# Setting the byte distance between the two operands of every matmul in a two-layer retention and gMLP block

## The chip, the cores and the metric

One NeuronCore of a Trainium2 chip runs the kernel in one launch. The metric is the device time of a whole execution in microseconds (us). The kernel before was timed three times: 915.23, 916.29 and 919.71 us, median 916.29 us.

## The reference

Two residual layers work on 512 latent tokens and 256 context tokens of width 1024. Layer 0 mixes tokens by bidirectional retention in four heads, layer 1 by a chunked gMLP; the result is the latent stream after a last RMSNorm. Cut to what matters:

```python
# layer 0
hx = rmsnorm(x, norm_g[0]) * (1 + scale_x) + shift_x      # hc the same from ctx
q, k, v, z = hx @ w_q, hx @ w_k, hx @ w_v, hx @ w_z       # rope on q, k
o = retention_forward(q, k, v) + retention_backward(q, k, v)   # states start from ctx
x = x + gate_x * ((rms(o) * silu(z)) @ w_out)
# layer 1
h = rmsnorm(x, norm_g[1]) * (1 + scale) + shift
u, v, z = h @ w_u, h @ w_v, h @ w_z
y = u * (w_s . normalised(v) + b_s) * silu(z)
x = x + gate * (y @ w_out);  return rmsnorm(x, final_g)
```

## The kernel before

**Precision.** TensorE takes float32r operands. Nearly every operand is kept as two halves, a rounded high part `h` and a low part `l`, side by side in one SBUF tile. `mm3` (L95) makes a product of three matmuls: low by high, high by low, high by high. In each matmul one operand is loaded into the array (the *stationary* operand, 128 columns, its own LDWEIGHTS in the trace) and the other streams past it (the *moving* operand, 256 or 512 columns). `split` (L101) makes the halves: ScalarE (ACT) copies the high part, VectorE (DVE) subtracts to get the low part.

**Projections.** The big products (q and k together, v, z, and u, v, z of layer 1) are cut in two by two blocks and multiplied with seven block products instead of eight (class `Product`, L298). The activations' blocks and their sums lie in seven 8 KB slots: A11, A12, A22, S1, S2, S3, S4 (tags `oA11` and so on). The context rows lie in a 16 KB slot `hc`. Class `Stream` (L125) brings the weights: it loads a raw block from HBM into a 4 KB slot (`w0` to `w7`, `g0` to `g3` and others, name `raw`), forms a difference where the scheme wants one (on DVE), and splits it into one of four 8 KB slots, tag `hl`. A block in `hl` is used by 24 matmuls, by 48 where the context rows are multiplied with it too.

`features` (L282), for q with k (`kq`) and for u with z (`u`), loads the weights `hl` into the array and streams the activations. `tokens` (L290), for v and z of layer 0 (`vz`) and v of layer 1 (`v1`), does it the other way round: the activations are stationary, the weights `hl` move.

**Retention.** `attend` (L917): `score` multiplies k (stationary) with q (moving, 256 wide) out of five 4 KB slots (name `qk`); `pv` takes the scores' halves `ph`, `pl` (2 KB slots, tag `t2`) as stationary operand and v (512 wide) as the moving one; v lies in the slots of A11, S1 and S2. `project_out` (L1005) has the output weights (`hl`) stationary and the gated result `og` moving; `og` lies in the slots of S3 and S4. `load_qk` (L826) brings q and k of the next head back from DRAM, each piece into a slot that a list of tags names.

**Layer 1's output.** `out1` (L1199) has the gated features stationary, `ya` in the slot `hc` and `yb` in `g2` and `g3`, and the weights `hl` moving, 512 wide.

**Where a tile lies.** Tiles come from one SBUF pool. A tag's slots get their address when the first tile with that tag is asked for, one behind the other, each rounded up to 32 bytes. So small tiles that are made early shift the start of all later ones.

**Order.** The text orders the work on TensorE (PE), ACT and DVE (class `Queue`, L38; through it every instruction of these engines has line L54 in the profile). SyncE (SP) issues all loads in one queue (L114), GpSimd (POOL) all stores to DRAM (L111).

Of the kernel before, what the change touches and what calls it, by code (L numbers as in the profile page):

```python
# [8 lines left out]
F32R = mybir.dt.float32r  # L9
# [4 lines left out]
P = 128  # L14
# [11 lines left out]
TW = XW + CW  # L26
# [41 lines left out]
def hybrid_kernel(ctx, tc, xT_d, cT_d, cv_d, sv_d, rows_d, ada0_d, adag_d, w_d, rope_d, dec_d, ws_d, id_d, out_d):  # L68
# [13 lines left out]
    def st(shape, tag, dt=F32, bufs=1, name=None):  # L82
        return sb.tile(shape, dt, tag=tag, name=name or tag, bufs=bufs)

    T2 = 11

    def t2(name, shape=(P, 512), dt=F32):
        return st(list(shape), "t2", dt, bufs=T2, name=name)

    def pt(shape=(P, 512), tag="ps"):  # L90
        return ps.tile(list(shape), F32, tag=tag, name="pst", bufs=6 if tag == "ps" else 2)
# [9 lines left out]
    def split(hl, src, late=None):  # L101
        h, l = hl
        act.copy(h, src)
        low = lambda: dve.tensor_tensor(l, src, f32(h), ALU.subtract)
        if late is None:
            low()
        else:
            late.append(low)
# [4 lines left out]
    def load(dst, src):  # L113
        nc.sync.dma_start(dst, src)  # L114


    USES = {"B11": ("11",), "B12": ("12",), "T1": ("12", "11"), "T2": ("22", "11"), "B21": ("21",), "T3": ("22", "12"),
            "B22": ("22",), "T4": ("21", "11")}
    AT = {"B11": "11", "B12": "12", "T1": "11", "T2": "11", "B21": "21", "T3": "12", "B22": "22", "T4": "21"}
    WITH = {"B11": "A11", "B21": "A12", "T1": "S1", "T2": "S2", "B22": "S4", "T3": "S3", "T4": "A22"}  # L120
    PAIRED = ("B11", "B21", "T1", "T2", "B22", "T3", "T4")
    SINGLE = ("B11", "T1", "T2", "B21", "T3", "B22", "T4")
    HL = 4

    class Stream:  # L125


# [37 lines left out]
        def upto(self, n, late=None):  # L165

            while self.done < min(n, self.limit or len(self.items)):
                q, name, uses, at, place = self.items[self.done]
                self.pump()
                raw = lambda u: self.raws[q, u]  # L170
                r = raw(at)
                if name[0] == "T":
                    dve.tensor_tensor(r, raw(uses[0]), raw(uses[1]), ALU.subtract)
                elif name[0] == "gated":
                    g = self.gate[:, name[1]:name[1] + 512].unsqueeze(1).to_broadcast([P, 2, 512])
                    rr = r.rearrange("p (e n) -> p e n", e=2)
                    dve.tensor_tensor(rr, rr, g, ALU.mult)
                hl = place() if place else st([P, 2, 1024], "hl", F32R, bufs=HL)
                split((hl[:, 0, :], hl[:, 1, :]), r, late)
                self.tiles[self.done] = hl  # L180
                self.done += 1
                if late is None:
                    self.drop(q, uses)
                else:
                    late.append(lambda: self.drop(q, uses))
# [89 lines left out]
    def op(key):  # L275
        A[key] = st([P, 2, 4, HS], "o" + key, F32R)
# [78 lines left out]
    cv = st([P, KT, 2], "cv")  # L355
# [47 lines left out]
    g0 = sv[:, 32:48].rearrange("p (k r) -> p k r", r=2)  # L403
    gateb0 = sv[:, 48:56]
    adab1 = sv[:, 56:72].rearrange("p (s k) -> p s k", s=2)
    g1 = sv[:, 72:80]
# [51 lines left out]
    def spread(s, name):  # L458

        pr = pt((P, HS), tag="tm")  # L460
        for i in range(2):
            mm(pr[:, i * P:i * P + P], s[:, 1, i:i + 1].to_broadcast([P, P]), ident, start=True, stop=True)
        rs = st([P, HS], name)
        act.copy(rs, pr)
        return rs
# [11 lines left out]
    def ada0_cols(kb, e):  # L477
        pq = pt((P, HS), tag="tm")
        for b in range(2):
            pe.transpose(pq[:, b * P:b * P + P], e[:, b * P:b * P + P], ident)  # L480
        s = st([P, 2, 2], "ada_s", bufs=2)
        v = pq.rearrange("p (b g r) -> p b r g", b=2, g=4)
        dve.tensor_reduce(s, v[:, :, 0:2, :], axis=AX.X, op=ALU.add)
        dve.tensor_tensor(gs0[:, kb, :], s[:, 0, :], adab0[:, 1, kb, :], ALU.add)
        dve.tensor_tensor(sh0[:, kb, :], s[:, 1, :], adab0[:, 0, kb, :], ALU.add)
        dve.scalar_tensor_tensor(gs0[:, kb, :], gs0[:, kb, :], 1.0, g0[:, kb, :], ALU.add, ALU.mult)

    hc = st([P, 2, KT, HS], "hc", F32R)
# [6 lines left out]
    rope = st([P, 2, SEQ], "rope")  # L495
# [53 lines left out]
    rs, sq = {}, {}  # L549

    def half_rows(src, g, s):
        for i in range(2):
            flips(src, g, i, s)
# [11 lines left out]
    def come(*what, then=None):  # L565


        made = []
        for kb, th in what:
            g, k = divmod(kb, 4)  # L570
            r = th // 2
            if r:
                f, h, l = cq[g][:, k, :], hc[:, 0, kb, :], hc[:, 1, kb, :]
            else:
                name = NAMES[th][g]
                if k == 0:
                    A[name] = st([P, 2, 4, HS], AT_S3.get(name, "o" + name), F32R)
                f, h, l = xq[th, g][:, k, :], A[name][:, 0, k, :], A[name][:, 1, k, :]
            dve.scalar_tensor_tensor(f, f, gs0[:, kb, r:r + 1], rs[th], ALU.mult, ALU.mult)
            made.append((f, sh0[:, kb, r:r + 1], h, l))  # L580
        if then:
            then()
        for f, b, h, l in made:
            act.activation(h, f, AF.Identity, bias=b, scale=1.0)
        for f, b, h, l in made:
            dve.scalar_tensor_tensor(l, f, b, f32(h), ALU.add, ALU.subtract)

    w0, bank = {}, {}

    def plain(kb, th, nhs=range(2)):  # L590

        g = kb // 4
        for nh in nhs:
            if th == 0 and kb % 4 == 0:
                w0[g, nh] = Q.get(ahead=0)
        if th == 2:
            if kb == 0:
                bank["c"] = pt()
            features(bank["c"], hc[:, :, 4 * g:4 * g + 4, :], w0[g, 0], g == 0, (kb % 4,))
            return  # L600
        for nh in nhs:
            if kb == 0:
                bank[th, nh] = pt()
            features(bank[th, nh], A[NAMES[th][g]], w0[g, nh], g == 0, (kb % 4,))
# [50 lines left out]
    for kb in range(1, 8):  # L655
        if kb == 3:
            Q.upto(4)
        plain(kb, 0)
        if kb + 1 < 8:
            ada0_cols(kb + 1, es)  # L660
            come((kb + 1, 0), (kb + 1, 1))
        if kb in (2, 6, 7):
            Q.upto({2: 3, 6: 5, 7: 6}[kb])
        plain(kb, 1)
        if kb + 2 < 8:
            es = ada0_mm(kb + 2)
        if kb == 2:
            ada0_load(6)
            ada0_load(7)
            Q.cap = None  # L670
            Q.pump()
        if kb in (2, 3):
            half_rows(rows_c, kb - 2, sq[2])
        if kb == 3:
            inverse(sq[2])
        if kb == 4:
            rs[2] = spread(sq[2], "rs2")
        come(*((k, 2) for k in CTX_COME.get(kb, ())))
        if kb == 7:
            hold((0, 0), (0, 1), (1, 0), (1, 1))  # L680
            op("S1")
            dve.tensor_tensor(f22, f21, f22, ALU.add)
            dve.tensor_tensor(shb, sh0[:, 0:4, 0], sh0[:, 4:8, 0], ALU.add)
            for k in range(4):
                shifted(f22[:, k, :], shb[:, k:k + 1], A["S1"][:, 0, k, :], A["S1"][:, 1, k, :])
        for k in CTX_PLAIN.get(kb, ()):
            plain(k, 2)
# [58 lines left out]
    gate0 = st([P, KT], "gate0")  # L746
# [77 lines left out]
        dve.tensor_tensor(l, f32(l), f32(h), ALU.subtract)  # L824

    def load_qk(h):  # L826
        tags = ("s0", "s1", "s2", "s3", "rope") if h % 2 == 0 else ("w4", "w5", "w6", "g2", "g3")
        srcs = (k_d[h][0], q_d[h][0], k_d[h][1], kc_d[h], q_d[h][1])
        t = []
        for tag, src in zip(tags, srcs):  # L830
            t.append(st([P, 2, 2, HS], tag, F32R, name="qk"))
            load(f32(t[-1][:, 1]).rearrange("p a b -> p (a b)"), src)
            if len(t) % 2:
                yield
        for x in t:
            halves(x)
            yield
        qk[h] = (t[1], t[4]), (t[0], t[2]), t[3]
        yield
# [3 lines left out]
    def load_wo(h):  # L843
        raws = []
        for c in range(4):
            for j in range(len(raws), min(c + 2, 4)):
                raws.append(st([P, 1024], ("w0", "w7")[j % 2], name="raw"))
                load(raws[j], w_d[16 * h + 12 + j])
            if c == 0:
                yield  # L850
            w = st([P, 2, 1024], "hl", F32R, bufs=HL)
            split((w[:, 0, :], w[:, 1, :]), raws[c])
            wos.setdefault(h, []).append(w)
            yield
# [554 lines left out]
```

## Time and profile before

| | |
|---|---|
| profiled execution: span from first to last instruction | 914.7 us |
| runs: median (lowest, highest) | 916.29 us (915.23, 919.71) |
| PE busy | 893.0 us, 98% of the span, 6872 matmuls |
| DVE busy | 722.8 us, 79% |
| ACT busy | 445.5 us, 49% |
| POOL busy | 51.5 us, 6% |
| TensorE clock granted | 0.997 |
| HBM traffic | 167 GB/s over the span |

The median of the runs is 1.6 us above the span of the profiled execution; that much lies around it or differs from run to run. A PE that is busy for 98% is not a PE at its peak: a matmul's record lasts from its start to its modelled end, and the next one starts long before that. What the stream costs is seen from start to start.

### The profile page before, as it was taken

Reading aid. Unit: us, or ns where it says so; the run is one execution under the profiler, and the core shown is the slowest. Engines: PE = TensorE matmul, PEld = TensorE weight load, DVE = VectorE, ACT = ScalarE, POOL = GpSimd, SP = SyncE. Lnnn points to the kernel's source line nnn. Section 1 sums busy time; section 2 is a strip of 40 time slices with the busy share of each in tenths; the row PEclk is TensorE's granted clock in tenths of the full one; section 3 lists DMA queues with packets and bytes.
Section 4 is the critical chain, followed back from the end, with each engine's and each line's share of the span. In section 5 each row is a group of like instructions: output and inputs, shape, how many; then the busy total and the mean of one; then the engine's idle time right before and its main releaser. Section 6 shows DMA issues by size and latency. Waiting matters only on the chain.

```text
span 914.7 us, 16952 instructions
## 1 busy us (share of the span) xinstructions
PE 893.0 (98%) x6872; PEld 846.9 (93%) x6872; DVE 722.8 (79%) x1024; ACT 445.5 (49%) x683; POOL 51.5 (6%) x88
## 2 busy tenths in 40 slices
PE   7999999999999998999999999999999999999997
PEld 6899999999999998998989889999999899899885
DVE  2689977698779866778666759999899489689985
ACT  5464634434545434636264448744545435244244
POOL 0001201101102011000000001011000000000000
PEclk9999999999999999999999999999999999999999
DMA  9943957456666367747254502536335135037102
GB/s 331 387 133 111 315 193 253 150 193 207 209 222 221 126 219 257 273 137 257 102 163 138 184 29 88 176 125 214 133 116 168 39 116 185 24 116 246 54 24 93
DMA packets 76782, 153.81 MB, mean 168 GB/s; under 512 B 7840, under 2 KB 34592, under 8 KB 76704
## 3 DMA queue, kind: packets, MB, share of 16 engines
q1 hardware_dynamic: 69840, 130.70, 43.3%
q0 software_dynamic: 6720, 22.03, 6.4%
q8 instruction: 54, 0.88, 0.4%
q14 instruction: 24, 0.20, 0.1%
q10 hardware_dynamic: 144, 0.01, 0.0%
HBM read 128.58 MB, written 24.12 MB: 167 GB/s over the span
## 4 chain that ended last, share of the span: by engine, by line
PE 82%; DVE 8%; DMA 4%; ACT 3%; issue 2%; SPq 1%; DVEq 0%; ACTq 0%
PE pst L54 82%; DVE hl L54 2%; DVE raw L54 2%; DVE ya L54 1%; DMA acc<-in_xT_dram 1%; DMA xq<-in_xT_dram 1%; ACT hl L54 1%; DMA raw<-in_w_dram 1%; SPq L114 1%; DMA vt<-vt 1%; ACT f L54 1%; ACT junk L54 0%; ACT oA L54 0%; DVE snap L54 0%; DVE bns L54 0%
## 5 line engine op out<-in xcount | busy, mean ns | idle before, releaser
L54 DVE TENSOR_TENSOR hl<-raw,hl 128x1024 fp32r<-128x1024 f32 x195 | 236.5, 1220 | 66.9 <-ACT hl L54 65.8
L54 ACT CAST hl<-raw 128x1024 fp32r<-128x1024 f32 x195 | 202.8, 1049 | 140.5 <-DVE raw L54 67.8
L54 PE MATMUL pst<-oS,hl 128*128 128x256 f32 x1104 | 136.1, 281 | 2.4 <-DVE hl L54 1.8
L54 PE MATMUL pst<-hl,oS 128*128 128x256 f32 x1152 | 137.6, 280 | 0.2 <-DVE snap L54 0.2
L54 PEld LDWEIGHTS pst<-hl,oS 128*128 128x128 f32 x1152 | 136.0, 188 | 1.3 <-ACT snap L54 0.8
L54 PEld LDWEIGHTS pst<-oS,hl 128*128 128x128 f32 x1104 | 132.3, 188 | 4.4 <-ACT ya L54 2.1
L54 PE MATMUL pst<-oA,hl 128*128 128x256 f32 x936 | 120.0, 284 | 0.2
L54 PEld LDWEIGHTS pst<-oA,hl 128*128 128x128 f32 x936 | 114.5, 189 | 2.5 <-DVE raw L54 0.8
L54 DVE TENSOR_TENSOR raw<-raw 128x1024 f32<-128x1024 f32 x92 | 111.3, 1219 | 0.8
L54 PE MATMUL pst<-hl,oA 128*128 128x256 f32 x816 | 100.3, 281 | 0.0
L54 ACT COPY snap<-pst 128x512 f32<-128x512 f32 x92 | 53.8, 585 | 95.0 <-PE pst L54 94.7
L54 PEld LDWEIGHTS pst<-hl,oA 128*128 128x128 f32 x816 | 98.0, 189 | 0.1
L54 PE MATMUL pst<-og,hl 128*128 128x256 f32 x768 | 93.7, 282 | 0.0
L54 PEld LDWEIGHTS pst<-og,hl 128*128 128x128 f32 x768 | 91.6, 188 | 0.9 <-DVE acc L54 0.2
L54 PE MATMUL pst<-hl,ya 128*128 128x512 f32 x288 | 70.3, 395 | 2.2 <-DVE ya L54 2.2
L54 PEld LDWEIGHTS pst<-hl,ya 128*128 128x128 f32 x288 | 53.8, 188 | 15.4 <-DVE ya L54 2.6
L54 PE MATMUL pst<-v,ph 128*128 128x512 f32 x192 | 60.9, 398 | 0.0
L54 DVE TENSOR_TENSOR snap<-pst,snap 128x512 f32<-128x512 f32 x69 | 47.2, 684 | 4.9 <-PE pst L54 4.3
L54 ACT CAST ph<-pf 128x512 fp32r<-128x512 f32 x24 | 14.9, 621 | 71.8 <-DVE pf L54 69.1
L54 PE MATMUL pst<-hl,hc 128*128 128x256 f32 x384 | 48.6, 282 | 0.0
L54 PEld LDWEIGHTS pst<-hl,hc 128*128 128x128 f32 x384 | 47.1, 188 | 0.0
L54 PEld LDWEIGHTS pst<-v,ph 128*128 128x128 f32 x192 | 36.6, 191 | 7.9
(171 smaller groups left out, 972.8 us busy)
## 6 DMA issues: line engine op xcount, KB each, us to landing
raw<-in_w_dram SPq DMA_DIRECT2D x224, 256.0 KB, 4.2
bg<-in_adag_dram SPq DMA_DIRECT2D x32, 512.0 KB, 4.0
ada_w<-in_ada_dram SPq DMA_DIRECT2D x16, 512.0 KB, 9.0
raw<-in_w_dram SPq DMA_DIRECT2D x16, 512.0 KB, 4.3
bg<-in_dec_dram SPq DMA_DIRECT2D x12, 512.0 KB, 4.3
v<-snap POOLq DMA_DIRECT2D x16, 256.0 KB, 4.7
z<-snap POOLq DMA_DIRECT2D x16, 256.0 KB, 4.2
v<-v SPq DMA_DIRECT2D x8, 512.0 KB, 4.0
```

Source lines behind the costliest of these rows:

```text
L54: made = op(*args, **kw)
L114: nc.sync.dma_start(dst, src)
```

## The change

Before the first tile is asked for, a loop asks for one tile of nearly every large tag and never uses it. This fixes the address of each slot. The four `hl` slots become 64 floats wider (2112), and a split weight block is put 8, 24 or 32 floats into its slot, by its kind. The small tile `rs2` moves into the slot `dec`. For heads 1 and 3, `load_qk` names its five slots in another order.

```diff
     T2 = 11
+    HL = 4
+    FORMS = {"kq": 8, "u": 8, "wo": 8, "vz": 24, "v1": 24, "o": 32}
+
+
+    for tag, size, bufs in (("hl", 2112, HL), ("t2", 512, T2), ("cv", 16, 1),
+                            *((f"o{k}", 2048, 1) for k in ("A11", "A12", "A22", "S1", "S2", "S3", "S4")), ("hc", 4096, 1),
+                            *((k, 1024, 1) for k in ("g2", "g3", "s0", "s2", "s3", "w4")), ("gate0", 8, 1),
+                            *((k, 1024, 1) for k in ("s1", "rope", "w5", "w6", "w0", "w1", "w2", "w3", "w7", "g1", "g0")), ("dec", TW, 1)):
+        st([P, size], tag, bufs=bufs, name="room")
+
+    def split_tile(form):
+        room = st([P, 2112], "hl", F32R, bufs=HL)
+        at = FORMS[form]
+        return room[:, at:at + 2048].rearrange("p (s n) -> p s n", s=2)
...
-    HL = 4
-
...
-                hl = place() if place else st([P, 2, 1024], "hl", F32R, bufs=HL)
+                hl = place() if place else split_tile(q[0])
...
-            rs[2] = spread(sq[2], "rs2")
+            rs[2] = spread(sq[2], "dec")
...
-        tags = ("s0", "s1", "s2", "s3", "rope") if h % 2 == 0 else ("w4", "w5", "w6", "g2", "g3")
+        tags = ("s0", "s1", "s2", "s3", "rope") if h % 2 == 0 else ("w4", "w5", "g2", "g3", "w6")
...
-            w = st([P, 2, 1024], "hl", F32R, bufs=HL)
+            w = split_tile("wo")
```

The addresses of the two built programs, start of the data modulo 256 bytes:

| operand | before | after |
|---|---|---|
| `hl` for kq, u, wo | 192 | 160 |
| `hl` for vz, v1 | 192 | 224 |
| `hl` for o (layer 1's output) | 192 | 0 |
| A11 (and v) | 192 | 192 |
| A12 | 32 | 192 |
| A22, S1, S2, S4 (and v, og) | 160 | 192 |
| S3 (and og) | 224 | 192 |
| `hc` (context, ya) | 96 | 192 |
| `g2`, `g3` (yb) | 160 | 192 |
| `ph`, `pl` | 128 | 128 |
| k of a head | 32 or 160 | 192 |
| q of a head | 32, 96 or 160 | 224 |

All steps inside these tiles are multiples of 512 bytes, so each matmul has one distance, the start of its moving operand less that of its stationary one, modulo 256. Counted over the float32r matmuls of the two programs:

| width | distance before | matmuls | which | distance after |
|---|---|---|---|---|
| 256 | 0 | 696 | A11 with `hl`; part of the scores | 32 |
| 256 | 32 | 1848 | S1, S2, S4, A22 stationary with `hl` moving; `hl` stationary with S3 moving | 32 |
| 256 | 96 | 696 | `hc` stationary with `hl` moving; `hl` stationary with A12 moving | 32 |
| 256 | 128, 192 | 72 and 72 | scores | 32 |
| 256 | 160 | 480 | `hl` stationary with `hc` moving; A12 stationary with `hl` moving | 32 |
| 256 | 224 | 1824 | `hl` stationary with S1, S2, S4, A22 moving; S3 stationary with `hl` moving | 32 (48 of them 0) |
| 512 | 32 | 288 | v in S1, S2 (192 matmuls); `yb` (96) | 64 |
| 512 | 64 | 96 | v in A11 | 64 |
| 512 | 96 | 288 | `ya` | 64 |

The instructions of PE, ACT, DVE and POOL are the same and stand in the same order. On SP two places move. The first is the loading of q and k of head 1 (`kc` is the context's k, `k` and `q` the latent tokens' halves; the buffer numbers are 30 higher after the change, since the loop makes 30 more tiles). The rows of the kernel before:

```order
55 L114 DMA qk<-kc_142 128x512
56 L114 DMA raw<-in_w_dram 128x2x256 x4
57 L114 DMA qk<-q_128 128x512
58 L114 DMA gateb_5178<-in_rows_dram 128x1024
64 L114 DMA bg<-in_dec_dram 128x1024
65 L114 DMA qk<-k_136 128x512
```

The same rows of SP in the changed kernel:

```order
55 L128 DMA qk<-k_166 128x512
56 L128 DMA raw<-in_w_dram 128x2x256 x4
57 L128 DMA qk<-kc_172 128x512
58 L128 DMA gateb_5208<-in_rows_dram 128x1024
64 L128 DMA bg<-in_dec_dram 128x1024
65 L128 DMA qk<-q_158 128x512
```

The second half of head 1's k (k_136, now k_166) is loaded first, the context's k second, and the second half of its q last. The other place on SP is the first raw blocks of layer 1's v (v1), which go into slots as these come free. The rows of the kernel before, with buffer numbers:

```order
178 L114 DMA raw_6149<-in_w_dram 128x2x256
179 L114 DMA raw_6158<-in_w_dram 128x2x256 x2
180 L114 DMA raw_6164<-in_w_dram 128x2x256 x2
181 L114 DMA raw_6179<-in_w_dram 128x2x256 x2
182 L114 DMA raw_6182<-in_w_dram 128x2x256 x2
```

The same rows in the changed kernel:

```order
178 L128 DMA raw_6179<-in_w_dram 128x2x256
179 L128 DMA raw_6209<-in_w_dram 128x2x256
180 L128 DMA raw_6194<-in_w_dram 128x2x256 x2
181 L128 DMA raw_6209<-in_w_dram 128x2x256
182 L128 DMA raw_6188<-in_w_dram 128x2x256 x2
183 L128 DMA raw_6212<-in_w_dram 128x2x256 x2
```

raw_6158 (now raw_6188) goes behind its two neighbours, because its slot `w6` now holds the piece of q of head 3 that is used longest.

## Prediction

> **What bounds the kernel now.** I read the page of the profile first: the span, the busy shares, the chain that ended last, and the groups.
>
> ```profile
> span 914.7 us, 16952 instructions
> PE 893.0 (98%) x6872; PEld 846.9 (93%) x6872; DVE 722.8 (79%) x1024; ACT 445.5 (49%) x683; POOL 51.5 (6%) x88
> ...
> PE 82%; DVE 8%; DMA 4%; ACT 3%; issue 2%; SPq 1%; DVEq 0%; ACTq 0%
> ...
> L54 PE MATMUL pst<-hl,oS 128*128 128x256 f32 x1152 | 137.6, 280 | 0.2 <-DVE snap L54 0.2
> ...
> L54 PEld LDWEIGHTS pst<-hl,oS 128*128 128x128 f32 x1152 | 136.0, 188 | 1.3 <-ACT snap L54 0.8
> ```
>
> The chain is PE for 82% of the span: 0.82 x 914.7 = 750 us of matmuls that follow each other, out of 893.0 us in which PE is busy. A factor of 750/893 = 0.84 will stand below for the share of the matmul stream that sets the end. One matmul lasts 280 ns and one weight load 188 ns, so at each moment the weights of the next matmul are read while the moving operand of the current one streams. Then I asked for the waits of PE, longest first:
>
> ```profile
> PE pst L54 <- DVE pl L54: 2.5, 2, 2.0
> PE pst L54 <- DVE pf L54: 2.4, 1, 2.4
> PE pst L54 <- DVE ya L54: 2.2, 1, 2.2
> PE pst L54 <- DVE hl L54: 1.8, 2, 1.4
> ```
>
> PE waits 8.9 us for DVE in the whole span. So the time is the number of matmuls by the pace at which one follows the other, and the change touches only that pace. The next view is the timeline of PE, whose rows give where a run of matmuls starts; the start of the next row less this one, by the count, is the pace. First, in the projections of layer 0, where products with different slots follow each other without a wait (columns: start and length in us, engine, operation, tiles; behind the arrow the moving tile stands first, then the stationary one; which of the A or S slots it is follows from the order of the block products in the kernel):
>
> ```profile
> 254.01 3.04 PE L54 MATMUL pst<-oA,hl 128*128 128x256 f32 x24
> 256.89 3.01 PE L54 MATMUL pst<-hc,hl 128*128 128x256 f32 x24
> 259.74 5.80 PE L54 MATMUL pst<-oS,hl 128*128 128x256 f32 x48
> 265.38 3.00 PE L54 MATMUL pst<-oA,hl 128*128 128x256 f32 x24
> 268.22 3.03 PE L54 MATMUL pst<-hl,oA 128*128 128x256 f32 x24
> 271.09 3.04 PE L54 MATMUL pst<-hl,hc 128*128 128x256 f32 x24
> 273.96 1.21 PE L54 MATMUL pst<-hl,oS 128*128 128x256 f32 x9
> ```
>
> These are equal instructions on equal shapes within 20 us, and the pace differs by the slot. A12 (distance 96 in the table of the change): 2.88/24 = 120.0 ns. `hc` moving (160): 2.85/24 = 118.8. S3 and S4 together (32 and 224): 5.64/48 = 117.5. A22 (224): 2.84/24 = 118.3. A11 (0): 2.87/24 = 119.6. `hc` stationary (96): 2.87/24 = 119.6. A long run with distance 32 alone (S1, S2, S4 stationary) and, a little before it, A12 stationary (160):
>
> ```profile
> 72.03 2.98 PE L54 MATMUL pst<-hl,oA 128*128 128x256 f32 x24
> 74.85 3.04 PE L54 MATMUL pst<-hl,hc 128*128 128x256 f32 x24
> ...
> 83.42 16.73 PE L54 MATMUL pst<-hl,oS 128*128 128x256 f32 x142
> ```
>
> Distance 32: (16.73 - 0.28)/141 = 116.7 ns, the 0.28 being the last matmul's own length. Check: half at 116.7 and half at 118.3 make 117.5, which is what S3 with S4 took. Distance 160 a second time: 2.82/24 = 117.5; I take 118.1, between the two rows. The distance 32 of the first rows has 224 and 192 as the two starts, that of the long run 192 and 160, and both kinds come out alike: the difference counts, not the place.
>
> The 512-wide matmuls: two steps of `pv`, first with v in A11 (distance 64), then with v in S1 (32), and layer 1's output with `ya` (96) and with `yb` and `ya` by turns:
>
> ```profile
> 404.84 0.40 PE L54 MATMUL pst<-v,pl 128*128 128x512 f32 x1
> ...
> 407.61 1.58 PE L54 MATMUL pst<-qk 128*128 128x256 f32 x12
> 409.02 0.40 PE L54 MATMUL pst<-v,pl 128*128 128x512 f32 x1
> ...
> 411.83 1.58 PE L54 MATMUL pst<-qk 128*128 128x256 f32 x12
> ```
>
> ```profile
> 707.87 22.56 PE L54 MATMUL pst<-hl,ya 128*128 128x512 f32 x96
> 730.26 1.00 PE L54 MATMUL pst<-oA,hl 128*128 128x256 f32 x7
> ```
>
> ```profile
> 773.64 1.57 PE L54 MATMUL pst<-hl,yb 128*128 128x512 f32 x6
> ...
> 796.05 3.03 PE L54 MATMUL pst<-oA,hl 128*128 128x256 f32 x24
> ```
>
> A `pv` step is 12 matmuls: 2.77/12 = 230.8 ns at distance 64, 2.81/12 = 234.2 at 32. `ya` at 96: 22.39/96 = 233.2. `yb` and `ya` by halves: 22.41/96 = 233.4, so `yb` at 32: 233.6.
>
> **The change part by part.** The counts are those of the table of distances.
>
> *256 wide, to distance 32 (116.7 ns).* From 0: 696 x 2.9 ns = 2.0 us. From 96: 696 x 3.1 = 2.2. From 160: 480 x 1.4 = 0.7. From 224: 1776 x 1.6 = 2.8. From 128 and 192 (144 matmuls of the scores) I have no clean row; by the ends of the others it is between 0 and 2.9 ns each, I take the middle, 0.2 us. The 48 that go from 224 to 0 lose 1.3 ns each, 0.1 us. The 1848 that have 32 already stay. Together 7.8 us.
>
> *512 wide, to distance 64 (230.8 ns).* v in S1 and S2: 192 x 3.4 = 0.7 us. `ya`: 288 x 2.4 = 0.7. `yb`: 96 x 2.8 = 0.3. v in A11 stays. Together 1.6 us (before rounding). The 64 is shown for `pv` alone; for `ya` and `yb`, which are 1.0 us of this, the least is nothing.
>
> The stream is shorter by 9.4 us. Of this the share on the chain counts, 0.84 x 9.4 = 7.9 us; the rest falls where DVE, ACT or a load sets the end and becomes a longer wait.
>
> A rule of the Trainium skill speaks against all of this. "TensorE: Matmul & The Clock Gate", Part 2, on what each phase of a matmul is for, says that TensorE has two independent SBUF read ports, one for the streaming operand and one for the weight load, so that loading the next weights takes nothing from the running matmul. By it the sum would be 0 and not 9.4. The rows above do not agree: 116.7 to 120.0 ns for the same instruction, by the distance of the two reads.
>
> *DVE and ACT.* Their operands move too. In the trace of before the two largest groups of DVE work on different pairings of slots:
>
> ```profile
> L54 DVE TENSOR_TENSOR hl<-raw,hl 128x1024 fp32r<-128x1024 f32 x195 | 236.5, 1220 | 66.9 <-ACT hl L54 65.8
> L54 DVE TENSOR_TENSOR raw<-raw 128x1024 f32<-128x1024 f32 x92 | 111.3, 1219 | 0.8
> ```
>
> 1220 and 1219 ns: DVE does not feel the address. I put 0. ACT is busy for 49% and has no more to lose.
>
> *DVE as the next bound.* What hides behind PE today is DVE, above all in two stages (columns: window, its length, busy time of PE, weight loads, DVE, ACT, POOL with instruction counts, clock, DMA):
>
> ```profile
> 75.00:110.00 35.00, 35.00 (x301) 35.00 (x300) 34.43 (x52) 21.35 (x27) 7.67 (x12) 1.00 0.66 215
> 560.00:640.00 80.00, 78.59 (x668) 78.19 (x667) 77.32 (x104) 47.84 (x70) 10.25 (x19) 1.00 0.48 159
> ```
>
> DVE has 0.57 us of slack in the first 35 us and 2.7 in the next 80. PE's gain there is 9.4/893 = 1.06%, so 0.4 and 0.8 us: it fits, barely. If all of it became waits, 1.2 us would be lost. That is a lower bound, not my value.
>
> *SP.* Head 1's k_136 now goes first, and SP waits for its store before the raw loads behind it. And raw_6158 goes behind its two neighbours. POOL's store, SP's load of that moment, the eight raw loads, and the ACT cast that reads raw_6158:
>
> ```profile
> 214.97 0.66 POOL L111 DMA_DIRECT2D k<-rope_a  x1
> ```
>
> ```profile
> 282.18 0.34 SPq L114 DMA_DIRECT2D qk<-kc  x1
> ```
>
> ```profile
> 515.36 6.73 SPq L114 DMA_DIRECT2D raw<-in_w_dram  x8
> ```
>
> ```profile
> 551.54 1.05 ACT L54 CAST hl<-raw 128x1024 fp32r<-128x1024 f32 x1 [0.97 <-PE pst L54]
> ```
>
> The store leaves 67 us before SP asks for it. raw_6158 stays among these eight loads, so it is issued by 515.36 + 6.73 = 522.1, 29 us before it is read. Both cost 0. The 30 unused tiles have no instruction; `rs2` in `dec` has long been read when the decay table comes there. 0.
>
> Sum: 914.7 - 7.9 = 906.8 us of span. The runs' median lies 1.6 us above the profiled span, so 916.3 - 7.9 = 908.4 us.
>
> Bounds of this case: least gain (9.4 - 1.0 - 0.2) x 0.84 - 1.2 = 5.7 us, so 910.6; most, all of 9.4 and 0.2 more for the scores on the chain, 906.7.
>
> **The rivals.** A measurement of this kernel can tell about 0.5%, 4.6 us, from no change; 911.7 and 920.9 are the bounds.
>
> *DVE takes the gain.* Where DVE is nearly full, a faster PE only waits. For it: the 98% and 97% above. Against it: in these 115 us PE hardly waits today. If DVE set the pace from 75 to 110 and from 560 to the end, 390 of 914.7 us, 390 x 1.06% = 4.1 us of the 9.4 go; (9.4 - 4.1) x 0.84 = 4.5, so 911.8 us.
>
> *The distance is not what counts.* The pace could go with something that runs beside PE in each product. Then nothing changes: 916.3 us. The Trainium skill's two independent ports (the page named above) would give this time too. Against it: the seven rows from 254 to 274 us have the same work beside them, and distance 96 gives 120.0 and 119.6 with different tiles in different roles.
>
> *PE's reads against other engines' writes: slower.* ACT, DVE and the DMAs write `hl`, `raw` and `t2` while PE reads. If PE's surcharge came from those writes, then the new layout, with every activation slot at 192, could put all pairs at the worst pace in the rows, 119.8. Today's mean over 5688 matmuls of 256 columns is 118.1; 5688 x 1.7 ns = 9.7, by 0.84 8.1 us: 924.4 us. It decides as soon as the mean pace of the 256-wide matmuls comes out above 118.1 ns. Against it: the long run at 116.7 has ACT and DVE writing `hl` all the time (DVE is full there).
>
> **How the numbers follow.** Forecast 0.75, DVE takes the gain 0.10, no change 0.10, slower 0.05. The range takes in the forecast's own 906.7 to 910.6, widened by about 1 us below because the three runs of before lie from 915.2 to 919.7, and reaches up past DVE's 911.8: 905.5 to 912.5. Left out are no change and slower, 0.15. Faster by over 0.5% (below 911.7): nearly all of the forecast and half of DVE's case, 0.79. Slower: 0.05. Within: 0.16.
>
> **What would show it.** In the changed profile each undisturbed 256-wide product of 24 should start 2.80 us before the next, whatever its slots, the run of 96 with `ya` should take 22.2 us, and DVE's subtraction into `hl` 1220 ns as now. PE's waits for DVE should grow from 8.9 us by at most 1 or 2; by 4 or more, DVE has taken the gain. Rows that still differ by slot between 116.7 and 120.0 would prove the reason wrong, also if the time falls.

## The result and the profile after

The changed kernel takes 911.88 us (median of 16 runs, 908.94 to 918.29) against 917.88 us for the kernel before (16 runs, 915.23 to 920.03): a ratio of 0.9941, with an interval of 0.9923 to 0.9959. By that ratio it is faster by about 5.4 us; the forecast was 7.9. The two medians lie 6.0 us apart and the profiled spans 4.7: 914.7 us before, 910.0 after.

The page of the changed kernel, the lines that answer to those of before:

```profile
span 910.0 us, 16953 instructions
PE 886.6 (97%) x6872; PEld 840.4 (92%) x6872; DVE 722.4 (79%) x1024; ACT 445.5 (49%) x683; POOL 51.5 (6%) x88
...
PE 61%; DVE 20%; DMA 7%; ACT 5%; issue 5%; SPq 1%; DVEq 0%; ACTq 0%
...
L54 DVE TENSOR_TENSOR hl<-raw,hl 128x1024 fp32r<-128x1024 f32 x195 | 236.7, 1222 | 65.5 <-ACT hl L54 64.8
```

PE is busy 6.4 us less, DVE as before, and one DVE subtraction lasts as before (1222 against 1220 ns). But the chain that ended last now goes through PE for 61% of the span, not 82%: DVE, DMA and ACT have come onto it.

**The pace.** The timeline of PE in the projections of layer 0, the same products as those shown of before:

```profile
253.89 2.96 PE L54 MATMUL pst<-hc,hl 128*128 128x256 f32 x24
256.69 5.76 PE L54 MATMUL pst<-oS,hl 128*128 128x256 f32 x48
262.29 2.96 PE L54 MATMUL pst<-oA,hl 128*128 128x256 f32 x24
265.09 2.96 PE L54 MATMUL pst<-hl,oA 128*128 128x256 f32 x24
267.89 2.96 PE L54 MATMUL pst<-hl,hc 128*128 128x256 f32 x24
```

Each of these products of 24 now starts 2.80 us before the next, 116.7 ns for a matmul, whatever slots it reads; before they took 2.82 to 2.88 us. The 512-wide matmuls, a `pv` run and layer 1's output with `ya`:

```profile
403.04 0.39 PE L54 MATMUL pst<-v,pl 128*128 128x512 f32 x1
403.27 0.63 PE L54 MATMUL pst<-v,ph 128*128 128x512 f32 x2
...
404.42 0.39 PE L54 MATMUL pst<-v,pl 128*128 128x512 f32 x1
...
703.12 22.15 PE L54 MATMUL pst<-hl,ya 128*128 128x512 f32 x96
725.11 2.96 PE L54 MATMUL pst<-oA,hl 128*128 128x256 f32 x24
```

1.38 us for six of `pv`, 230.0 ns, and 21.99/96 = 229.1 ns with `ya` (233.2 before).

These paces do not hold everywhere in the changed kernel. Two products with `hl` moving past S1 and S2, at distance 32 like all the others, and a later run of 96 of layer 1's output, at distance 64 like the one above:

```profile
323.31 5.82 PE L54 MATMUL pst<-hl,oS 128*128 128x256 f32 x48
328.97 2.99 PE L54 MATMUL pst<-hl,oA 128*128 128x256 f32 x24
...
768.68 1.56 PE L54 MATMUL pst<-hl,yb 128*128 128x512 f32 x6
...
791.09 2.99 PE L54 MATMUL pst<-oA,hl 128*128 128x256 f32 x24
```

The first take 5.66/48 = 117.9 ns; the same two products took 5.61/48 = 116.9 before, when they had distance 32 too. The output takes 22.41/96 = 233.4 ns, no less than before the change, and so does the run of 96 behind it. One distance can have two paces. The mean over the 256-wide matmuls that follow each other without a wait fell from 118.1 to 116.9 ns.

**Where the gain went.** The n-th matmul is the same in both programs, so its start after less its start before, each from the span's start, says how much has been won up to there. The last column adds only the pairs of matmuls that follow each other without a wait in both traces; it is what the pace alone has given so far.

| time in the trace of before | start of the matmul, after less before | from the pace alone |
|---|---|---|
| 110 us | -1.24 us | -0.94 us |
| 334 us | -3.45 | -3.56 |
| 366 us | -5.81 | -3.68 |
| 508 us | -6.30 | -4.86 |
| 541 us | -4.51 | -5.01 |
| 686 us | -5.76 | -5.88 |
| 895 us | -4.48 | -7.73 |
| 908 us | -4.72 | -7.97 |

The pace gives 8.0 us by the end and keeps giving. The time follows it to 686 us, with a jump each way at 345 to 366 and 520 to 541 that nearly cancel. From 686 to 895 us, in layer 1, the pace gives 1.85 us more and the kernel loses 1.28: here 3.1 us are taken by something else. The waits of PE from 680 to 890 us, before:

```profile
PE pst L54 <- DVE ya L54: 2.2, 1, 2.2
PE pst L54 <- DVE hl L54: 0.4, 1, 0.4
```

and after (total, times, longest):

```profile
PE pst L54 <- DVE hl L54: 2.8, 3, 1.6
PE pst L54 <- DVE ya L54: 2.4, 1, 2.4
```

So PE waits 2.4 us more there for a weight block that DVE splits. (Over the whole kernel it is 3.7 against 1.8 us, 1.9 more: a wait near 669 us became shorter.) In the chain of before this stretch was one piece:

```profile
691.83 187.20 PE pst L54 x1304
```

In the chain of the changed kernel it is broken:

```profile
687.21 43.67 PE pst L54 x280
...
732.47 1.24 DVE hl L54
734.63 4.62 DMA vt<-vt
...
752.82 44.10 PE pst L54 x280
```

`vt` is v of layer 1, which comes back from DRAM for the next block of u and is scaled by DVE (`load_vt`). DVE at this place, with its idle time in brackets, first before the change:

```profile
743.10 1.40 DVE L54 TENSOR_SCALAR vt<-vt,mv,rv 128x256 f32<-128x256 f32 x4 [0.51 <-DMA vt<-vt]
```

and after:

```profile
737.55 0.74 DVE L54 TENSOR_SCALAR vt<-vt,mv,rv 128x256 f32<-128x256 f32 x2 [0.36 <-DMA vt<-vt]
739.28 0.74 DVE L54 TENSOR_SCALAR vt<-vt,mv,rv 128x256 f32<-128x256 f32 x2 [0.98 <-DMA vt<-vt]
```

And SP's queue:

```profile
729.42 4.64 SPq L128 DMA_DIRECT2D raw<-in_w_dram  x5
734.15 0.86 SPq L128 DMA_DIRECT2D vt<-vt  x2
```

The load of `vt` is issued behind five raw loads and needs about 4.6 us from there. DVE comes to the scaling first, stands 1.34 us (0.51 before), and everything that DVE does behind it, the split of the next weight blocks among it, is later by that much. PE feels it at 752.82. DVE stood in front of this load before the change too: over layer 1 these waits of DVE add up to 9.9 us before and 11.0 after.

My theory: the distance sets the pace, and what the forecast had too much is lost because the load of `vt` does not get faster with PE. The rivals: something that runs beside PE sets the pace; or DVE is simply full, and would take the gain wherever it came from.

### The profile page after: what moved, and what is told of

The parts are those of the page before. It is cut to its first block, busy times and chain, and to the rows that moved or that the text cites. A ratio compares the mean times of both kernels' runs of the same rounds, so it can differ in the third digit from the quotient of the medians.

```text
span 910.0 us, 16953 instructions
## 1 busy us (share of the span) xinstructions
PE 886.6 (97%) x6872; PEld 840.4 (92%) x6872; DVE 722.4 (79%) x1024; ACT 445.5 (49%) x683; POOL 51.5 (6%) x88
## 4 chain that ended last, share of the span: by engine, by line
PE 61%; DVE 20%; DMA 7%; ACT 5%; issue 5%; SPq 1%; DVEq 0%; ACTq 0%
PE pst L54 61%; DVE hl L54 5%; DMA raw<-in_w_dram 4%; DVE raw L54 4%; DVE ya L54 2%; ACT hl L54 2%; DVE o L54 2%; DMA vt<-vt 2%; SPq L128 1%; DMA acc<-in_xT_dram 1%; DVE pf L54 1%; DMA xq<-in_xT_dram 1%; DVE snap L54 1%; DVE ada_a L54 1%; ACT junk L54 1%
## 5 line engine op out<-in xcount | busy, mean ns | idle before, releaser
L54 DVE TENSOR_TENSOR hl<-raw,hl 128x1024 fp32r<-128x1024 f32 x195 | 236.7, 1222 | 65.5 <-ACT hl L54 64.8
L54 PE MATMUL pst<-oA,hl 128*128 128x256 f32 x936 | 118.1, 281 | 0.2
L54 PEld LDWEIGHTS pst<-oA,hl 128*128 128x128 f32 x936 | 112.6, 188 | 2.6 <-DVE raw L54 0.8
L54 DVE TENSOR_TENSOR raw<-raw 128x1024 f32<-128x1024 f32 x92 | 111.5, 1221 | 0.8
```

Of the source, the lines that this page charges most:

```text
L54: made = op(*args, **kw)
```

## The experiments

**One matmul stream, nothing beside it.** The kernel `scan` leaves both layers out. It runs only float32r matmuls from slots that no other engine touches, in groups of 48 at 256 columns for each distance in steps of 8 bytes, then in groups of 24 at 512 columns.

```python
def group(d, n, count):
    off = (-d % 256) // 4
    ...
        w = weights[:, 1 if t == 0 else 0, off + 128 * k:off + 128 * k + 128]
        m = moved[:, 1 if t == 1 else 0, n * k:n * k + n]
        mm(bank[:, 0:n], w, m, start=i == 0, stop=i == count - 1, skip_group_check=True)
for d in range(0, 256, 8):
    group(d, 256, 48)
```

> Matmuls alone, no layers are computed: 32 groups of 48 matmuls of 256 columns, with the distance between moving and stationary operand going from 0 to 248 bytes in steps of 8, then 16 groups of 24 of 512 columns in steps of 16; ACT, DVE and the DMAs are idle meanwhile. If the distance alone sets the pace, the groups at 0, 32, 96, 128, 160, 192 and 224 bytes come out as in the full kernel: 119.5, 116.8, 119.8, 118.6, 118.1, 117.2 and 118.3 ns from start to start, and 512 wide 230.7 ns at 64 and 233 to 234 at 32 and 96; what lies between the multiples of 32, and 64 at 256 columns, is not known yet. If the surcharge comes from the writes of other engines, all groups have one pace, at or below 116.7 ns.

Its stretch of 256-wide groups shows that no other engine runs (PE, weight loads, DVE, ACT, POOL):

```profile
20.00:208.00 188.00, 188.00 (x1595) 188.00 (x1594) 0.00 (x0) 0.00 (x0) 0.00 (x0) 1.00 0.00 1
```

The groups at distances 0, 32, 168 and 192, and 512 wide at 0 and 32:

```profile
23.13 5.99 PE L91 MATMUL bank<-moved,weights 128*128 128x256 f32 x48
...
46.36 5.84 PE L91 MATMUL bank<-moved,weights 128*128 128x256 f32 x48
...
144.93 5.72 PE L91 MATMUL bank<-moved,weights 128*128 128x256 f32 x48
...
162.12 5.71 PE L91 MATMUL bank<-moved,weights 128*128 128x256 f32 x48
```

```profile
208.25 5.71 PE L91 MATMUL bank<-moved,weights 128*128 128x512 f32 x24
...
219.40 5.83 PE L91 MATMUL bank<-moved,weights 128*128 128x512 f32 x24
```

A group's length holds its first matmuls too, which are uneven. After six to eight matmuls the gaps repeat strictly, and the mean over each group's second half is:

| width | distance: ns from start to start |
|---|---|
| 256 | 0: 120.0, 32: 116.7, 64: 117.8, 96: 120.0, 128: 118.7, 160: 118.6, 168: 113.3, 192: 113.3, 224: 118.3, 232: 121.5, 248: 115.5 |
| 512 | 0 and 16: 226.7, 32: 233.3, 64: 228.9, 96: 233.3, 160: 234.3, others 230.0 to 233.3 |

At 0, 32, 96, 160 and 224 this is the pace that the full kernel shows; at 192 it is not, the scores' 117.2 ns against 113.3. The pace differs by distance with nothing beside PE; the rivals with work beside PE fall. `scan` moves the stationary operand alone, so it can't tell the distance from that operand's place. The rows of the kernel before can: there `hl` lies at 192 as the stationary operand and its products take 118.3 to 120.0 ns by where the moving one lies. And each distance ran here in one stretch only (0 also in the first groups), so a second pace of the same distance would not show. The Trainium skill ("TensorE: Matmul & The Clock Gate", Part 2, what each phase is for) has weights and streaming operand on independent SBUF read ports, so that one takes nothing from the other. These groups, equal in all but the distance, do not agree with it: 113.3 to 121.5 ns. What happens between the two reads no run here shows.

**All distances 0.** The changed kernel, with its split weight blocks 64 bytes into their slots, so that 5400 matmuls of 256 columns have distance 0:

```diff
-    FORMS = {"kq": 8, "u": 8, "wo": 8, "vz": 24, "v1": 24, "o": 32}
+    FORMS = {"kq": 16, "u": 16, "wo": 16, "vz": 16, "v1": 16, "o": 16}
```

> The changed kernel with every weight half put 16 floats into its slot, so that nearly all products with weights have distance 0; slots, order and all else as in the changed kernel. If the distance is the cause: 119.5 ns per 256-wide matmul instead of 116.9, 5350 x 2.6 = 14 us more in PE's stream, about 0.84 of it on the chain; against the kernel before, whose mean is 118.1, 5400 x 1.4 x 0.84 = 6 us slower, 920 to 923 us, ratio 1.007. If the new slots help for another reason than the distance: as the changed kernel, ratio 0.994.

922.93 us, a ratio to the kernel before of 1.0069 (1.0047 to 1.0091): slower than either, with the same instructions. The same products of layer 0:

```profile
259.27 3.04 PE L54 MATMUL pst<-hc,hl 128*128 128x256 f32 x24
262.15 5.92 PE L54 MATMUL pst<-oS,hl 128*128 128x256 f32 x48
```

2.88 us for 24, 120.0 ns (before: 2.85 for the first of these rows). What pays is the value of the distance, not that it is the same everywhere. And with PE at this pace no wait for `hl` is left in PE's waits: they are 0 here, 1.8 us in the kernel before and 3.7 in the changed one, so they grow as PE gets faster.

**The load of vt earlier, after and before.** `vt` is the changed kernel with the load asked for behind the first block product of a u block instead of the third; DVE's scaling stays where it was, in a function of its own, `scale_vt`. `b_vt` is the same edit on the kernel before.

```diff
             prod.run(name, Q.get())
-            if name == "T2" and i < UZ - 1:
+            if name == "B11" and i < UZ - 1:
                 load_vt(i + 1)
+            if name == "T2" and i < UZ - 1:
+                scale_vt(i + 1)
```

> The changed kernel with the load of layer 1's vt asked for at B11 of the block before instead of at T2, its scaling on DVE left at T2. If the late load holds DVE up and this is where layer 1 lost its gain: the waits of PE near 687, 752 and 819 us (1.9, 0.8, 0.9 us in the changed kernel) go, span 906 to 907 us, ratio 0.990. If DVE's own work fills the stage: the waits stay, span 910, ratio 0.994.

> The kernel before with the same earlier load of vt and nothing else. If the late load was hidden behind PE before the change: at most the two waits of PE near 669 and 691 us go (1.7 and 0.7 us), ratio 0.998 to 1.000. If DVE's own work fills the stage: no difference, 1.000. If the gain of the earlier load does not hang on the distance at all: the same 3 to 4 us as on the changed kernel, 0.996.

`vt`: 906.78 us, ratio 0.9889 (0.9868 to 0.9911). `b_vt`: 915.01 us, ratio 0.9973 (0.9959 to 0.9986). DVE in `vt` at the place shown above:

```profile
728.25 1.38 DVE L54 TENSOR_SCALAR vt<-vt,mv,rv 128x256 f32<-128x256 f32 x4
```

The scaling waits for nothing, and from 680 to 890 us PE waits for DVE only once, 2.2 us for the last `ya`. No wait for `hl` is left in `vt` or `b_vt`. `b_vt` itself decides little: its ratio lies between what was expected of a load hidden before the change (0.998 to 1.000) and of a gain that does not hang on the distance (0.996), and its interval holds values of both.

DVE has the same work as before, so a full DVE was not the cause. With the load early on both sides, the distances are worth 0.9889/0.9973 = 0.992 (0.989 to 0.994, the two half-widths added in squares; both kernels were compared with the same runs of the kernel before), 7.7 us of 917.47, near the forecast's 7.9. That they meet is in part luck: the mean granted clock is 0.9973 over the runs of `vt` and 0.9955 over those of `b_vt`, which by my estimate (the difference by a span of 910 us) is 1.7 us of the 7.7. The profiles show the same: ahead of its last 10 us `b_vt` has two stretches of 3.41 us at half the clock, `vt` one.

The early load itself is worth 2.5 us on the kernel before, by its ratio, and 4.8 on the changed one (0.9889 against 0.9941, the latter from another set of runs, so 4.8 with 2.6 either way). The difference, 2.3 us, is as large as the part of the forecast that was missing, but the runs can't show it: it is too small against its interval, and the runs of the changed kernel have a mean clock of 0.9946 (0.9960 in the set of the kernel before that `vt` and `b_vt` ran with), which by the same estimate is 2.5 of the 4.8 us. The traces show it more surely: the early load takes away 3.7 us of PE's waits for `hl` from the changed kernel and 1.8 from the kernel before, so 1.9 us of the gain were lost there.

**The distances at which the scan is fastest.** `d192` puts the weights so that 5352 matmuls of 256 columns have distance 192 and layer 1's output has 0; `d192_vt` has the early load as well. `d168_vt` does it for 168.

```diff
-    FORMS = {"kq": 8, "u": 8, "wo": 8, "vz": 24, "v1": 24, "o": 32}
+    FORMS = {"kq": 32, "u": 32, "wo": 32, "vz": 0, "v1": 0, "o": 16}    # d192, d192_vt
+    FORMS = {"kq": 38, "u": 38, "wo": 38, "vz": 58, "v1": 58, "o": 16}  # d168_vt
```

> The changed kernel with other places in the slot (32, 0 and 16 floats), so that 5352 matmuls of 256 columns have distance 192 and the 384 of layer 1's output distance 0, the best of the scan (113.3 and 226.7 ns after some 6 matmuls). If the distance sets the pace here as it does alone: 5352 x 3.6 = 19 us and 384 x 4 = 1.5 us less in PE's stream than in the changed kernel; part of it is lost on DVE with the late vt load, so 896 to 902 us, ratio 0.977 to 0.983. If the low pace needs long undisturbed runs (the scores, in runs of 12, had 117.2 at this distance): as the changed kernel, 0.994.

> The same places with the earlier load of vt. If the distance sets the pace: 0.84 x 20.5 = 17 us less than the changed kernel with the earlier load, 889 to 894 us, ratio 0.970 to 0.975. If DVE becomes the bound all over: a few us less only, 900 us, 0.981. If the low pace is not reached: 0.989.

> Distance 168 instead of 192 for the 256-wide products with weights (places 38 and 58 floats; no multiple of 32 bytes), with the earlier load of vt. In the scan 168 and 192 had the same pace, 113.3 ns. If the distance alone counts: the same time as with 192. If starts off a multiple of 32 bytes cost ACT or DVE something: DVE's subtraction into hl above 1220 ns and a longer time than with 192.

`d192`: 911.81 us, ratio 0.9931 (0.9908 to 0.9954). `d192_vt`: 904.14 us, 0.9849 (0.9814 to 0.9883), the fastest kernel here. `d168_vt`: 910.25 us, 0.9911 (0.9880 to 0.9942). The 889 to 894 us expected of `d192_vt` were missed, since the pace of 113.3 ns came only in part. Products of `d192_vt`:

```profile
202.16 2.99 PE L54 MATMUL pst<-hl,hc 128*128 128x256 f32 x24
204.99 5.82 PE L54 MATMUL pst<-hl,oS 128*128 128x256 f32 x48
...
268.57 2.88 PE L54 MATMUL pst<-hl,hc 128*128 128x256 f32 x24
271.29 5.60 PE L54 MATMUL pst<-hl,oS 128*128 128x256 f32 x48
```

and of `d168_vt`:

```profile
256.72 2.88 PE L54 MATMUL pst<-hc,hl 128*128 128x256 f32 x24
259.44 5.60 PE L54 MATMUL pst<-oS,hl 128*128 128x256 f32 x48
...
270.46 3.04 PE L54 MATMUL pst<-hl,hc 128*128 128x256 f32 x24
273.34 5.90 PE L54 MATMUL pst<-hl,oS 128*128 128x256 f32 x48
```

At 192 the same product with the same tiles takes 2.83 us at 202 us and 2.72 at 268: 117.9 or 113.3 ns. A pace is kept through many products and changes where the kind of product does; the kind alone does not fix it. At 168 the products with the activations moving (2.72 us) show 113.3 ns here, those with the weights moving (2.88) 120.0. The means over the 256-wide matmuls are 116.4 and 117.6 ns (117.1 in `vt`). DVE's subtraction takes 1221 ns in `d168_vt`, so starts off a multiple of 32 bytes cost it nothing. `d192` without the early load, with 5.5 us of PE's waits for `hl`, is level with the changed kernel (0.9931 against 0.9941), and with it `d192_vt` stands at 0.9849 against 0.9889 for `vt`, with intervals that overlap. What decides between the paces at one distance stays open.

## Why the prediction was right, and where it was off

- *The paces of 256 columns.* Right to the decimal in most products: 116.7 ns forecast for distance 32, and 2.80 us for an undisturbed product of 24, whatever its slots. The step from one distance to one pace was too simple: some products took 117.8 ns at the same distance, so that the mean came to 116.9. The sign named for a wrong reason, rows that still differ by slot, did not come: these rows differ by time, not by slot.
- *512 wide to 230.8 ns at distance 64, also for `ya`, which was not shown.* Right for the `pv` run shown, 230.0, and for the first run of layer 1's output, 229.1. The second and third, 233.4 and 233.3, won nothing, which the lower bound of the forecast had allowed for.
- *9.4 us of stream.* 8.0 us are seen in pairs without a wait on either side. Part of the rest is the second pace, which the sum did not know; the other pairs can't be compared one by one.
- *DVE and ACT at 0, SP's moved loads at 0.* Right for DVE (1222 ns, 722.4 us busy). No wait for the loads that the change moved stands among PE's waits.
- *"It fits, barely", 75 to 110 and 560 to 640 us.* Right in both stages. DVE fills them still more (the third window is layer 1):

```profile
75.00:110.00 35.00, 35.00 (x302) 35.00 (x301) 34.78 (x53) 21.73 (x28) 7.67 (x12) 1.00 0.69 218
560.00:640.00 80.00, 78.70 (x671) 78.25 (x670) 78.11 (x108) 47.15 (x65) 10.79 (x20) 1.00 0.49 165
680.00:890.00 210.00, 204.80 (x1429) 189.94 (x1428) 169.35 (x223) 88.27 (x121) 0.00 (x0) 1.00 0.33 106
```

From 60 to 110 us, by the same matching of matmuls as in the table, the pace gives 0.56 us and the start of the matmuls moves by 0.56; from 600 to 661 us it is 0.53 and 0.52. Nothing was taken here.
- *The factor 0.84, 7.9 us.* This is the term that was mis-sized: of the 9.4 us of stream 5.4 came by the ratio of the runs, a factor of 0.57 in place of 0.84, and 4.7 in the traces. The share of the old chain says where the stream set the end before; it can't say what is late next. The forecast looked for the next bound where an engine is nearly full, and it came in layer 1, where DVE is busy for 169 of 210 us: the load of `vt`, issued at a fixed place of SP's order, lands when it lands, and DVE stands in front of it with the splits queued behind. This cost 1.9 us of waits for `hl`. With that load early in both kernels the distances are worth 7.7 us, or about 6 at an equal granted clock by the estimate above, so the factor stays below 0.84 even then. In the traces 8.0 us of pace became 4.7 of span; what the rest of these 3.3 us went to was not followed, beyond the two jumps. The four groups of waits that the prediction added up to 8.9 us grew to 10.6, within the bound that it named, since others of them became shorter; the sum alone would not have shown it. (They are not all of PE's waits for DVE, though the prediction takes them so: three smaller groups add 1.6 us before.)
- *The rival "DVE takes the gain".* Its 911.8 us is almost the result, and its stretch from 560 us to the end holds layer 1, but the way is another: where DVE was nearly full (99% and 98% of the two windows) nothing was lost, and in layer 1, with a fifth of its time free, it was held up by a load.
- *"The distance is not what counts" and "against other engines' writes".* Both fall with `scan`, and with `d0`, whose pace gets worse while everything beside PE is the same.

## What to carry to other kernels

Where matmuls follow each other without a wait, take the pace from start to start for each pairing of slots; if equal instructions differ, the addresses of the two operands are a thing to set. A matmul-only kernel like `scan` shows in one run which distances are slow; its best pace need not hold in the kernel (at 192, 113.3 ns alone and a mean of 116.4 in the kernel). Before a faster stream is called won, go through the transfers whose place in a queue is fixed and that someone already waits for, however shortly: they do not speed up with it, and an engine with a fifth of its time free can still be held up by one.

## What the runs showed of the hardware

**Pace and distance.** Without any other engine the pace at 256 columns lies between 113.3 and 121.5 ns by the distance modulo 256 bytes, at 512 between 226.7 and 234.3. It sets in after six to eight matmuls and then repeats strictly; in the kernels 32, 168 and 192 have more than one steady pace at 256 columns (116.7 or 117.8 ns at 32), and 64 has two at 512 (229.1 and 233.4).

**The clock after a wait.** The jumps of the table at 345 to 366 and 520 to 541 us are neither pace nor vt. PE's longest waits for DVE in the changed kernel (total, times, longest; of before they stand in the prediction):

```profile
PE pst L54 <- DVE hl L54: 3.7, 4, 1.6
PE pst L54 <- DVE pl L54: 3.1, 2, 2.1
...
PE pst L54 <- DVE pf L54: 1.4, 1, 1.4
```

The longest for `pl` and the one for `pf` lie in attention. Windows behind them, before (behind the five busy times stands the granted clock; `pl` first, then `pf`):

```profile
527.90:532.00 4.10, 4.01 (x22) 3.47 (x23) 1.23 (x3) 1.88 (x6) 0.00 (x0) 1.00 0.41 128
352.00:356.50 4.50, 4.49 (x19) 3.91 (x20) 3.77 (x6) 2.29 (x4) 0.00 (x0) 0.62 0.39 130
```

and after, behind `pl`:

```profile
522.00:526.30 4.30, 4.30 (x13) 3.35 (x14) 1.10 (x2) 0.84 (x3) 0.00 (x0) 0.63 0.37 121
```

Behind its wait of 2.4 us for `pf` the kernel before has a granted clock of 0.62 (0.50 from 353.06 to 356.47 us), and behind the one of 2.0 us for `pl` none is lost. The changed kernel has 0.63 behind its 2.1 us for `pl`; its wait for `pf` is 1.0 us shorter, which is part of the first jump. Which wait is hit differs between the two traces, and the span goes with it: over the 16 runs of the changed kernel, time and mean granted clock have a correlation of -0.82 (0.998 at 908.94 us, 0.990 at 918.29). The Trainium skill ("TensorE: Matmul & The Clock Gate", Part 1) puts the half clock behind at least one idle window of about 3.4 us. The half clock is there in these windows, but behind waits of 2.1 to 2.4 us. The length of the wait alone does not decide: behind a wait of 2.9 us for `pf` in `d0` the clock stays at 1.00. That these waits cause the spread of the runs was not tried by taking them away.
